# Loading the first layer's modulation weights by row blocks, four column groups at a time

## The chip, the cores and the metric

The kernel runs on one core of a Trainium2 chip. The metric is the time of one execution in microseconds of the device, median over runs. TensorE is called PE, VectorE DVE, ScalarE ACT, GpSimd POOL; SP (SyncE) computes nothing and issues most DMA transfers.

## The reference, cut to what matters

Two layers of a hybrid of attention, convolution and a linear recurrence over 1024 latent tokens, with a prefix of 256 context tokens, model width 1024. Only the entry of the first layer is touched:

```python
shift, scale, gate = split(silu(c) @ w_ada[0] + b_ada[0], 3)            # for the latent tokens
shift_c, scale_c, gate_c = split(silu(c_ctx) @ w_ada[0] + b_ada[0], 3)  # for the context
h  = layer_norm(x)   * (1 + scale)   + shift
hc = layer_norm(ctx) * (1 + scale_c) + shift_c
... = split_in_proj(h @ w_in[0])        # and the same of hc; gates: sigmoid(h @ w_gate + b_gate)
```

`w_ada[0]` is 1024 x 3072, all in 32-bit floats. The entry needs its first 2048 columns (shift and scale); the last 1024 are computed later, beside other work.

## The kernel before

Every product with `h` is done as three products of parts: `h` is cut into `hi` and `lo` (`hchi`, `hclo` for the context, `hlhi`, `hllo` for the latent tiles), each weight tile into `whi` (by ACT) and `wlo` (by DVE), and hi x hi, lo x hi, hi x lo are summed in PSUM. `h` is held transposed, model width on the partitions, in eight tiles of 128: `NT_C` (256 context tokens), `NT_0` and `NT_1` (512 latent tokens each).

`emit_h0` (L424) makes the first `h`. Its list `order` (L488) sets the sequence: `("a", g, q)` loads a block of `w_ada`, 256 rows by 512 columns (L437), and multiplies it with `cs`, the two vectors silu(c) and silu(c_ctx) as columns, into a PSUM tile `pa` of two rows (`ada_rows`, L442); after the fourth block of a column group `ada_fin` copies the two rows to SBUF (`arow`), turns them with 16 small matmuls in all against `sel`, and adds the bias into `ada[0]`. `("r",)` loads the eleven parameter rows (`load_rows`, L256) in SP's queue. `("x", i)` loads a tile of 128 tokens and normalizes it (`norm_x`: statistics on DVE, the power on POOL, `nb` on DVE, the scaling on ACT). `("m", nt, j)` modulates four of the eight tiles of `nt` (`modulate`, L459): transposes into `p0`, ACT writes `hf` with scale and shift, then `hi` by ACT or DVE, and `lo` by DVE.

`wcols` (L328) loads a weight of 1024 x 128 columns as 128 x 8 x 128, so in pieces of 512 B, and cuts it.

Behind `emit_h0` the streams of a layer (recurrence, attention, convolution, gates) are merged by a planner, `Driver`, which runs them by modelled costs and by the times at which it believes a thing ready. The tile framework then orders each engine's instructions, and the result is a fixed order on each engine. An engine takes its instructions in that order; a DMA queue too: an issue that waits holds up all that is behind it. DMA transfers share eight semaphores, taken in turn, so an issue also waits until an earlier transfer of the same semaphore has landed.

Of the kernel before, what the change touches and what calls it, by code (L numbers as in the profile page):

```python
# [17 lines left out]
D = 1024  # L18
# [21 lines left out]
LEAD = (2.0, 3.0, 1.5, 2.0)  # L40
SLACK = (1.0, 5.0, 2.0, 2.0)
MARGIN = (1.0, 3.0, 1.5, 0.0)
HOP = (0.2, 0.4, 0.1, 0.15)
PRIO = ((0, 1, 7, 3, 4, 5, 6, 8, 2), (1, 2, 8, 0, 4, 3, 6, 5, 7))
ROOM_SCORES = (3, 6)
# [144 lines left out]
def kernel(  # L190
# [23 lines left out]
    pad(H, 448, "padh1")  # L214
    pad(SM, 32, "pads")
    PR = ctx.enter_context(tc.tile_pool(name="padr", bufs=1, side="right"))
    pad(PR, 320, "padr")

    def f32(ap):
        return ap.bitcast(F32)  # L220
# [32 lines left out]
    P_ADA, P_GATE, P_CB, P_CG, P_CLB, P_LCW, P_LCB, P_BA, P_BX, P_LAM = 0, 24, 48, 52, 56, 60, 92, 100, 108, 116  # L253
    prm, cwt, drv = [], [], []

    def load_rows(l, get):  # L256
        ra, rb = get(), get()
        dve.memset(ra[96:128], 0.0)
        dve.memset(rb[96:128], 0.0)
        for off, n, src in (  # L260
            (P_ADA, 24, b_ada[l].rearrange("(r p) -> r p", p=128)),
            (P_GATE, 24, b_gate[l].rearrange("(r p) -> r p", p=128)),
            (P_CB, 4, conv_dw_b[l].rearrange("(r p) -> r p", p=128)),
            (P_CG, 4, conv_ln_g[l].rearrange("(r p) -> r p", p=128)),
            (P_CLB, 4, conv_ln_b[l].rearrange("(r p) -> r p", p=128)),
            (P_LCW, 32, lru_conv_w[l].rearrange("d k (r p) -> (d k r) p", p=128)),
            (P_LCB, 8, lru_conv_b[l].rearrange("d (r p) -> (d r) p", p=128)),
            (P_BA, 8, lru_b_a[l].rearrange("d (r p) -> (d r) p", p=128)),
            (P_BX, 8, lru_b_x[l].rearrange("d (r p) -> (d r) p", p=128)),
            (P_LAM, 8, lru_lambda[l].rearrange("d (r p) -> (d r) p", p=128)),  # L270
        ):
            sp.dma_start(out=ra[off:off + n], in_=src)
        sp.dma_start(out=rb[0:CK * 4], in_=conv_dw_w[l].rearrange("k (r p) -> (k r) p", p=128))
        return ra, rb

    def load_params(l, ra, rb):
# [65 lines left out]
    def wroom(n=1):  # L342
        return lambda: wlive[0] + n <= NW

    def wcols(src, o):
        return Wt(src[:, o:o + 128].rearrange("(k p) n -> p k n", p=128), KD, 128)
# [2 lines left out]
        act.activation(out=hi, in_=src, func=AF.Copy)  # L349
        dve.tensor_tensor(out=lo, in0=src, in1=f32(hi), op=ALU.subtract)  # L350

    cs = K.tile([128, KD, 2], F32, tag="cs", name="cs")
    csr = K.tile([128, KD, 4], F32R, tag="csr", name="csr")
    sel = K.tile([4, 2], F32, tag="sel", name="sel")
    dve.tensor_tensor(out=sel, in0=ident[0:4, 0:2], in1=ident[0:4, 2:4], op=ALU.add)

    def load_c():
        rows = SM.tile([128, 128], F32, tag="crow", name="crow")
        sp.dma_start(out=rows[0:8], in_=c[0].rearrange("(r p) -> r p", p=128))
        sp.dma_start(out=rows[8:16], in_=c_ctx.rearrange("(r p) -> r p", p=128))  # L360
# [58 lines left out]
    hT = {}  # L419

    def alloc_h(ti, n):
        tg, b = ("hc", 2) if n == 256 else ("hl", 4)
        return tuple(H.tile([128, KD, n], F32R, tag=tg, name=f"{tg}{v}", bufs=b) for v in ("hi", "lo"))

    def emit_h0(R, P):
        tiles = [(ctxt, 0), (ctxt, 128)] + [(x, 128 * i) for i in range(8)]
        raws, xt = {}, {}
        nts = (NT_C, NT_0, NT_1)

        def load_x(i):  # L430
            t = R.tile([128, 2, 512], F32, tag="raw0", name="x0", bufs=17).rearrange("p a b -> p (a b)")
            sp.dma_start(out=t, in_=tiles[i][0][0, tiles[i][1]:tiles[i][1] + 128, :])
            xt[i] = t

        def load_ada(g, q):
            raws[g, q] = R.tile([128, 2, 512], F32, tag="raw0", name="raw0", bufs=17)
            sp.dma_start(out=raws[g, q], in_=w_ada[0][q * 256:q * 256 + 256, g * 512:g * 512 + 512].rearrange(  # L437
                "(k p) n -> p k n", p=128))

        rows_ = {}  # L440

        def ada_rows(g, q):  # L442
            if q == 0:
                rows_[g] = P.tile([128, 512], F32, tag="p0", name="pa", bufs=4)
            for k in range(2):
                pe.matmul(out=rows_[g][0:2], lhsT=cs[:, q * 2 + k, :], rhs=raws[g, q][:, k, :],
                          start=(q == 0 and k == 0), stop=(q == 3 and k == 1))
            if q == 3:
                ada_fin(0, [g * 4 + i for i in range(4)], rows_[g], 2,
                        R.tile([128, 512], F32, tag="hf0", name="arow", bufs=5))  # L450
# [8 lines left out]
        def modulate(j, nt):  # L459
            ti, t0, n = nt  # L460
            s = 1 if ti == 0 else 0
            ps = P.tile([128, 512], F32, tag="p0", name="p0", bufs=4)
            for i in range(n // 128):
                pe.transpose(ps[:, i * 128:i * 128 + 128], xt[t0 // 128 + i][:, j * 128:j * 128 + 128], ident)
            hf = R.tile([128, 512], F32, tag="hf0", name="hf0", bufs=5)
            act.activation(out=hf[:, 0:n], in_=ps[:, 0:n], func=AF.Identity, scale=ada[0][:, 8 + j, s:s + 1],
                           bias=ada[0][:, j, s:s + 1])
            hi, lo = (v[:, j, :] for v in hT[0, ti])
            if j < (4, 4, 6)[ti]:
                act.activation(out=hi, in_=hf[:, 0:n], func=AF.Copy)  # L470
            else:
                dve.tensor_copy(hi, hf[:, 0:n])
            dve.tensor_tensor(out=lo, in0=hf[:, 0:n], in1=f32(hi), op=ALU.subtract)

        load_c()
        for nt in nts:
            hT[0, nt[0]] = alloc_h(nt[0], nt[2])
            if nt is NT_C:
                pad(H, 64, "padh2")

        def rows_tile():
            return R.tile([128, 128], F32, tag="rows", name="rows", bufs=2)

        order = [("a", 0, 0), ("a", 0, 1), ("a", 0, 2), ("r",), ("a", 2, 0), ("a", 0, 3), ("a", 2, 1), ("a", 2, 2),
                 ("a", 2, 3), ("x", 0), ("x", 1), ("a", 1, 0), ("a", 1, 1), ("a", 1, 2), ("a", 1, 3), ("a", 3, 0),
                 ("a", 3, 1), ("a", 3, 2), ("a", 3, 3), ("m", NT_C, 0), ("m", NT_C, 4), ("x", 2), ("x", 3),
                 ("x", 4), ("x", 5), ("x", 8), ("m", NT_0, 0), ("m", NT_0, 4), ("x", 6), ("x", 9), ("x", 7),
                 ("m", NT_1, 0), ("m", NT_1, 4)]  # L488
        for what, *v in order:
            if what == "m":  # L490
                for j in range(v[1], v[1] + 4):
                    modulate(j, v[0])
            elif what == "r":
                load_params(0, *load_rows(0, rows_tile))
            elif what == "a":
                load_ada(*v)
                ada_rows(*v)
            else:
                load_x(*v)
                norm_x(*v)  # L500

    class Pool_:

# [14 lines left out]
    def both(*conds):  # L518
        return lambda: all(c() for c in conds)

    def phase1(l, R, RH):
# [14 lines left out]
        def gemm_nt(w, nt, evac, wide=False):  # L536
            ti, t0, n = nt
            if wide and not state["lru"]:
                yield ("pe", w.ready)
                ps = psum2()  # L540
            else:
                yield ("pe", w.ready, lambda: pl_.used < (2 if state["lru"] else 3))
                pl_.take()
                wide = False
                ps = psum()
# [46 lines left out]

        def lru_in():
            for cc in range(4):
                yield ("pe", both(lambda: xgo[0] >= cc, wroom(), sl.room(), hl_.room(3)))
                w = wcols(w_in[l], O_XL + cc * 128)
                sl.take()
                hl_.take(3)
                lw_raw = half("lw_raw")
# [476 lines left out]

                yield from gating(0, j, get, 1.0)

        gorder = list(range(16, 24)) + list(range(8, 16)) + list(range(8))

        def gate_nt(w, j, nt):
            yield ("pe", w.ready, hl_.room())
# [8 lines left out]
            hl_.give()  # L1091

        def gates():
            ws = {}

            def fetch(i):
                if i < len(gorder) and i not in ws:
# [351 lines left out]
```

## Time and profile before

| | us |
|---|---|
| median of 3 runs | 2331.7 (2331.32 to 2335.34) |
| the profiled execution | 2330.59 |
| its span | 2328.8 |
| PE busy | 2268.0 (97%) |
| DVE busy | 1748.5 (75%) |
| ACT busy | 1067.1 (46%) |
| first product with `h` on PE begins at | 54.67 |

The granted clock is the share of TensorE's 2.4 GHz that it was given: 1.00, or 0.50 at the lower of its two levels; a mean between them is a stretch with both. Windows give the busy time of each engine in a stretch with its number of instructions. A 32-bit matmul stands as two records in the trace. The recorded duration of a matmul is longer than its step, as matmuls are pipelined: from start to start is what one costs in a row.

### The profile page before, as it was taken

The page shows a single profiled execution, that of the slowest core. Times are in us where ns is not written, and L with a number is a line of the kernel's source. Part 1 is how long each engine was busy: PE and PEld are TensorE (multiplying, and loading weights), DVE is VectorE, ACT ScalarE, POOL GpSimd, SP SyncE. Part 2 cuts the span into 40 slices and gives each one's busy share as a digit, 9 for nine tenths or more (in the row PEclk, how much of TensorE's full clock was granted, in tenths as well). Part 3 has the DMA queues.
Part 4 walks back from the last instruction along what each step waited for, and adds up shares of the span by engine and source line. Part 5 has one row for each costly group of instructions (what it writes and reads, how often), then busy time and mean ns, then how long its engine had stood idle before and what let it go on. Part 6 is the DMA issues. An engine that isn't in the chain of part 4 may idle for free.

```text
span 2328.8 us, 32221 instructions
## 1 busy us (share of the span) xinstructions
PE 2268.0 (97%) x12253; PEld 1921.6 (83%) x12253; DVE 1748.5 (75%) x2588; ACT 1067.1 (46%) x1702; POOL 91.4 (4%) x140
## 2 busy tenths in 40 slices
PE   7999999999999999999999999999999999999998
PEld 3888888888888887888988888888888878778988
DVE  5579967869859874448888839979778787657786
ACT  4555563244444575323444535665344456543231
POOL 1000000000000111000101000000000011000000
PEclk8999999999999999999999999999999999999999
DMA  7222323433334232567565522223433334348482
GB/s 279 70 75 98 118 75 121 138 116 109 100 120 132 84 102 88 189 214 226 169 223 176 187 70 66 75 90 128 140 93 96 91 118 136 109 135 279 136 280 73
DMA packets 305820, 309.91 MB, mean 133 GB/s; under 512 B 20609, under 2 KB 239617, under 8 KB 305665
## 3 DMA queue, kind: packets, MB, share of 16 engines
q1 hardware_dynamic: 277152, 255.94, 34.8%
q10 hardware_dynamic: 28512, 51.92, 6.3%
q8 instruction: 96, 1.57, 0.3%
q14 instruction: 60, 0.48, 0.1%
HBM read 232.92 MB, written 74.87 MB: 132 GB/s over the span
## 4 chain that ended last, share of the span: by engine, by line
PE 88%; DVE 6%; ACT 3%; DMA 2%; issue 2%; SPq 0%; POOLq 0%; POOL 0%; ACTq 0%; DVEq 0%
PE ps L73 81%; PE yp L73 3%; PE pt L73 2%; PE pa L73 1%; DVE wlo L73 1%; DVE acc L73 1%; DVE P L73 1%; ACT whi L73 1%; DVE pl L73 1%; DMA qd<-qd 0%; DVE xp L73 0%; PE p L73 0%; DMA raw<-in_w_out_dram 0%; ACT hf L73 0%; DVE st L73 0%
## 5 line engine op out<-in xcount | busy, mean ns | idle before, releaser
L73 PE MATMUL ps<-hlhi,whi 128*128 128x512 f32 x1728 | 681.4, 395 | 2.4 <-DVE gs L73 1.0
L73 PE MATMUL ps<-hlhi,wlo 128*128 128x512 f32 x1728 | 677.0, 392 | 2.0 <-DVE wlo L73 2.0
L73 PE MATMUL ps<-hllo,whi 128*128 128x512 f32 x1728 | 678.0, 392 | 0.1
L73 ACT ACTIVATE whi<-raw 128x1024 fp32r<-128x1024 f32 x240 | 253.9, 1058 | 433.6 <-PE ps L73 393.0
L73 DVE TENSOR_TENSOR wlo<-raw,whi 128x1024 fp32r<-128x1024 f32 x240 | 293.9, 1224 | 124.1 <-ACT whi L73 121.5
L73 PEld LDWEIGHTS ps<-hlhi,wlo 128*128 128x128 f32 x1728 | 325.5, 188 | 70.5 <-DVE wlo L73 2.9
L73 PEld LDWEIGHTS ps<-hlhi,whi 128*128 128x128 f32 x1728 | 326.1, 189 | 67.1 <-DVE pl L73 2.0
L73 PEld LDWEIGHTS ps<-hllo,whi 128*128 128x128 f32 x1728 | 325.8, 189 | 62.9 <-issue 0.7
L73 DVE SCALAR_TENSOR_TENSOR acc<-u,cwt,acc 128x1296 f32<-128x1296 f32 (+1 forms) x240 | 342.6, 1427 | 2.1
L73 PE MATMUL ps<-yh,whi 128*128 128x512 f32 (+1 forms) x480 | 175.6, 372 | 7.1 <-DVE thl L73 4.9
L73 PE MATMUL ps<-yl,whi 128*128 128x512 f32 (+1 forms) x480 | 176.3, 369 | 1.4 <-DVE yl L73 1.4
L73 PE MATMUL ps<-yh,wlo 128*128 128x512 f32 (+1 forms) x480 | 176.6, 369 | 0.0
L73 ACT ACTIVATE ph<-pt 128x512 fp32r<-128x512 f32 x160 | 93.9, 591 | 128.5 <-PE pt L73 126.7
L73 DVE TENSOR_TENSOR pl<-pt,ph 128x512 fp32r<-128x512 f32 x160 | 109.1, 686 | 50.9 <-ACT ph L73 49.4
L73 PE MATMUL ps<-whi,hlhi 128*128 128x256 f32 x512 | 144.3, 284 | 0.0
L73 PE MATMUL ps<-wlo,hlhi 128*128 128x256 f32 x512 | 144.0, 283 | 0.0
L73 PE MATMUL ps<-whi,hllo 128*128 128x256 f32 x512 | 142.6, 283 | 0.0
L73 ACT ACTIVATE P<-P,nm 128x640 f32<-128x640 f32 (+1 forms) x128 | 101.9, 797 | 81.3 <-DVE nm L73 81.2
L73 PE MATMUL ps<-hchi,whi 128*128 128x256 f32 x480 | 136.0, 283 | 2.0 <-ACT hchi L73 0.8
L73 PE MATMUL ps<-hchi,wlo 128*128 128x256 f32 x480 | 135.6, 282 | 1.0 <-DVE wlo L73 1.0
L73 PE MATMUL ps<-hclo,whi 128*128 128x256 f32 x480 | 134.8, 281 | 0.0
L73 DVE CUSTOM_DVE_ANT_0 P<-ps,m_mid,nsink 128x640 f32<-128x640 f32 (+1 forms) x112 | 93.2, 860 | 42.2 <-PE ps L73 40.7
(207 smaller groups left out, 3753.2 us busy)
## 6 DMA issues: line engine op xcount, KB each, us to landing
raw<-in_w_in_dram SPq DMA_DIRECT2D x60, 512.0 KB
raw<-in_w_branch_dram SPq DMA_DIRECT2D x60, 512.0 KB
raw<-in_w_ada_dram SPq DMA_DIRECT2D x48, 512.0 KB
raw<-in_w_gate_dram SPq DMA_DIRECT2D x48, 512.0 KB
th<-tg ACTq DMA_DIRECT2D x96, 256.0 KB
thl<-th SPq DMA_DIRECT2D x96, 256.0 KB
raw<-in_w_out_dram SPq DMA_DIRECT2D x40, 512.0 KB
yd<-gs ACTq DMA_DIRECT2D x48, 256.0 KB
```

The lines of the kernel that those rows point to most:

```text
L73: return f(*a, **k)
```

## The change

- The modulation weights of the first layer come in eight row blocks of 128 rows by 2048 columns (1 MiB, 8 KB in one piece a row) in place of sixteen blocks of 256 by 512. `cs` is padded to 32 columns, and each block is multiplied by four matmuls that write partitions 0, 32, 64 and 96 of one PSUM tile `pa` (`tile_position`). One copy (`arow`), four transposes and four additions make `ada[0]`.
- The parameter rows and c, c_ctx are loaded from ACT's queue.
- The context tiles are loaded first; once normalized they are transposed into PSUM and wait there, unmodulated.
- All x tiles have their own buffers; each group's loads and normalizings stand ahead of the modulation of the group before. The cut of `hi` moves from ACT to DVE in more tiles: (0, 2, 4) of eight by ACT in place of (4, 4, 6).
- The first gate weight and the first weight of the recurrence are loaded in `emit_h0`; the planner is told that the latent halves are ready at 12 and 24.

```diff
-    def load_rows(l, get):
+    def load_rows(l, get, queue=None):
+        queue = queue or sp
...
-            sp.dma_start(out=ra[off:off + n], in_=src)
+            queue.dma_start(out=ra[off:off + n], in_=src)
...
-    cs = K.tile([128, KD, 2], F32, tag="cs", name="cs")
+    csz = K.tile([128, KD, 32], F32, tag="cs", name="cs")
+    dve.memset(csz, 0.0)
+    cs = csz[:, :, 0:2]
...
-        sp.dma_start(out=rows[0:8], in_=c[0].rearrange("(r p) -> r p", p=128))
+        act.dma_start(out=rows[0:8], in_=c[0].rearrange("(r p) -> r p", p=128))
...
-            if j < (4, 4, 6)[ti]:
+            if j < (0, 2, 4)[ti]:
...
-        order = [("a", 0, 0), ("a", 0, 1), ("a", 0, 2), ("r",), ("a", 2, 0), ("a", 0, 3), ("a", 2, 1), ("a", 2, 2),
...
+        ra, rb = load_rows(0, lambda: R.tile([128, 128], F32, tag="rows", name="rows", bufs=2), act)
+        for i in range(2):
+            load_x(i)
+        pa = psum(name="pa")
+        raws = []
+        for q in range(KD):
+            raws.append(R.tile([128, 2048], F32, tag="raw0", name="raw0", bufs=5))
+            sp.dma_start(out=raws[q], in_=w_ada[0][q * 128:q * 128 + 128, 0:2048])
+            for g in range(4):
+                pe.matmul(out=pa[32 * g:32 * g + 32], lhsT=csz[:, q, :], rhs=raws[q][:, g * 512:g * 512 + 512],
+                          start=(q == 0), stop=(q == KD - 1), tile_position=(0, 32 * g))
+            if q == 0:
+                load_params(0, ra, rb)
+            elif q == 1:
+                for i in range(2):
+                    norm_x(i)
+                cps = [turn(NT_C, j) for j in range(KD)]
+        row = hf_tile("arow")
+        act.activation(out=row, in_=pa, func=AF.Copy)
+        pr = psum(name="pr")
+        for i in range(4):
+            pe.transpose(pr[:, i * 128:i * 128 + 128], row[:, i * 128:i * 128 + 128], ident)
+        for g in range(4):
+            bias = prm[0][:, P_ADA + 4 * g:P_ADA + 4 * g + 4].unsqueeze(2).to_broadcast([128, 4, 2])
+            dve.scalar_tensor_tensor(out=ada[0][:, 4 * g:4 * g + 4, :],
...
+        first_w["gate"] = wcols(w_gate[0], GATES[0] * 128)
+        first_w["lru"] = wcols(w_in[0], O_XL)
+        for i in range(2, 6):
+            load_x(i)
+        for j in range(KD):
+            modulate(NT_C, j, cps[j])
+        for i in range(2, 6):
+            norm_x(i)
...
+        hr[0, 1], hr[0, 2] = 12.0, 24.0
...
-                yield ("pe", w.ready)
+                yield ("pe", w.ready, hr.get((l, ti), 0.0))
```

What stands on three queues is set by the framework, and the diff does not show it. SP's queue at the start, before (`raw0` are blocks of `w_ada`, `rows` the parameter rows):

```order
L437 DMA raw0_188<-in_w_ada_dram 128x2x512
L437 DMA raw0_193<-in_w_ada_dram 128x2x512
L437 DMA raw0_197<-in_w_ada_dram 128x2x512
L272 DMA rows_201<-in_b_ada_dram 24x128
L272 DMA rows_201<-in_b_gate_dram 24x128
L272 DMA rows_201<-in_conv_dw_b_dram 4x128
L272 DMA rows_201<-in_conv_ln_g_dram 4x128
L272 DMA rows_201<-in_conv_ln_b_dram 4x128
```

SP's queue around the last blocks, now (`x0` are tiles of tokens, `raw` the gate and input weights):

```order
L488 DMA raw0_296<-in_w_ada_dram 128x2048
L444 DMA x0_173<-in_x_dram 128x1024
L444 DMA x0_174<-in_x_dram 128x1024
L444 DMA x0_175<-in_x_dram 128x1024
L488 DMA raw0_302<-in_w_ada_dram 128x2048
L444 DMA x0_176<-in_x_dram 128x1024
L444 DMA x0_177<-in_x_dram 128x1024
L444 DMA x0_178<-in_x_dram 128x1024
L488 DMA raw0_308<-in_w_ada_dram 128x2048
L331 DMA raw_654<-in_w_gate_dram 128x8x128
L331 DMA raw_674<-in_w_in_dram 128x8x128
```

The rows have left SP's queue, and the last three weight blocks stand behind all tiles of x; a second pair of weights stands behind the last block. ACT where the modulation begins, before:

```order
L73 ACTIVATE arow_325<-pa_310 2x512
L73 ACTIVATE hf0_335<-p0_332,ada0_160 128x256
L73 ACTIVATE hf0_342<-p0_339,ada0_160 128x256
L73 ACTIVATE x0_388<-x0_388,nb_398,rs_395 128x1024
L73 ACTIVATE hf0_349<-p0_346,ada0_160 128x256
L73 ACTIVATE hchi_180<-hf0_335 128x256
L73 ACTIVATE hchi_180<-hf0_342 128x256
L73 ACTIVATE x0_401<-x0_401,nb_411,rs_408 128x1024
```

and now:

```order
L74 ACTIVATE x0_176<-x0_176,nb_512,rs_509 128x1024
L74 ACTIVATE x0_177<-x0_177,nb_523,rs_520 128x1024
L74 ACTIVATE x0_178<-x0_178,nb_534,rs_531 128x1024
L74 ACTIVATE whi_656<-raw_654 128x1024
L74 ACTIVATE arow_314<-pa_216 128x512
L74 ACTIVATE whi_676<-raw_674 128x1024
L74 ACTIVATE hf0_341<-p0_258,ada0_161 128x256
L74 ACTIVATE hf0_345<-p0_258,ada0_161 128x256
```

All normalizing (`x0<-x0`) now stands ahead of the first `hf`, and two weight cuts have come between. DVE at the same place, before:

```order
L73 BN_STATS st_442<-x0_440 128x6 x2
L73 SCALAR_TENSOR_TENSOR ada0_160<-pa_310,prm0_219 128x8
L73 SCALAR_TENSOR_TENSOR nb_424<-mv_419,rs_421 128x1
L73 TENSOR_SCALAR rs_434<-mv_432 128x1
L73 BN_AGGR mv_445<-st_442 128x2
L73 TENSOR_TENSOR hclo_181<-hf0_335,hchi_180 128x256
```

and now:

```order
L74 TENSOR_TENSOR wlo_657<-raw_654,whi_656 128x1024
L74 TENSOR_TENSOR wlo_677<-raw_674,whi_676 128x1024
L74 SCALAR_TENSOR_TENSOR ada0_161<-pr_316,prm0_226 128x8 x4
L74 CAST hchi_191<-hf0_341 128x256
L74 TENSOR_TENSOR hclo_192<-hf0_341,hchi_191 128x256
```

The additions that make `ada` stood among the statistics of x; now they stand behind the low parts of the two weights.

## Rows read from the trace of the kernel before

**Rows 1.** PE's waits, 60 to 1100 us: total, times, longest; first and last of eleven.
```profile
PE yp L73 <- ACT ph L73: 6.3, 6, 2.2
...
PE ps L73 <- ACT arow L73: 0.2, 1, 0.2
```
**Rows 2.** Windows: length, busy PE, PEld, DVE, ACT, POOL, granted clock, DMA share, GB/s.
```profile
40.00:50.00 10.00, 5.60 (x28) 3.41 (x28) 7.89 (x25) 9.96 (x16) 1.80 (x4) 0.71 0.62 208
50.00:60.00 10.00, 8.28 (x47) 7.52 (x47) 7.98 (x23) 10.00 (x15) 2.29 (x3) 0.61 0.54 156
```
**Rows 3.** Timeline of PE: start, duration, operation, tiles, form, records [idle before].
```profile
13.63 7.03 PE L73 MATMUL pa<-raw,cs 128*2 128x512 f32 x16
...
53.05 1.97 PE L73 MATMUL p<-ident,x 128*128 128x128 f32 x8 [1.72 <-ACT hf L73]
54.67 0.57 PE L73 MATMUL ps<-hchi,whi 128*128 128x256 f32 x1
...
58.00 0.28 PE L73 MATMUL ps<-hchi,wlo 128*128 128x256 f32 x1
58.12 0.28 PE L73 MATMUL ps<-hchi,whi 128*128 128x256 f32 x1
...
59.54 1.03 PE L73 MATMUL p<-ident,x 128*128 128x128 f32 x8
60.33 0.36 PE L73 MATMUL ps<-hchi,whi 128*128 128x256 f32 x1
...
68.14 0.40 PE L73 MATMUL ps<-hlhi,wlo 128*128 128x512 f32 x1
68.37 0.39 PE L73 MATMUL ps<-hlhi,whi 128*128 128x512 f32 x1
```
**Rows 4.** PE's groups, 42 to 80 us; second and third stand for three each.
```profile
L73 PE MATMUL p<-ident,x 128*128 128x128 f32 x73 | 14.2, 332 | 5.8 <-ACT hf L73 3.9 <-ACT x L73 1.9
L73 PE MATMUL ps<-hchi,whi 128*128 128x256 f32 x24 | 7.4, 308 | 0.0
...
L73 PE MATMUL ps<-hlhi,whi 128*128 128x512 f32 x16 | 6.4, 403 | 0.0
```
**Rows 5.** Windows by what moved: weights, the hole, weights, tiles, gate weights.
```profile
3.70:7.80 4.10, 2.06 (x4) 0.52 (x5) 0.84 (x4) 1.27 (x3) 0.00 (x0) 1.00 1.00 374
7.80:11.20 3.40, 3.40 (x7) 0.51 (x5) 0.00 (x0) 0.00 (x0) 0.00 (x0) 1.00 0.16 34
20.00:30.00 10.00, 10.00 (x36) 3.35 (x35) 3.75 (x14) 2.96 (x3) 1.07 (x2) 1.00 1.04 388
32.00:38.00 6.00, 6.00 (x23) 2.06 (x22) 2.70 (x7) 0.01 (x1) 0.00 (x0) 1.00 1.03 406
38.50:41.50 3.00, 2.69 (x14) 1.19 (x12) 3.00 (x11) 1.46 (x4) 1.25 (x3) 1.00 1.21 303
```
**Rows 6.** Timeline of SP's queue: start, duration, what was issued.
```profile
1.18 0.37 SPq L359 DMA_DIRECT2D crow<-in_c_dram  x1
1.93 1.42 SPq L437 DMA_DIRECT2D raw<-in_w_ada_dram  x3
```
**Rows 7.** Timeline of DVE, columns as in Rows 3.
```profile
20.30 1.29 DVE L73 BATCH_NORM_STATS2 st<-x 128x6 f32<-128x512 f32 x2 [0.64 <-DMA x<-in_ctx_dram]
...
45.78 0.29 DVE L73 CAST hchi<-hf 128x256 fp32r<-128x256 f32 x1
...
47.51 1.22 DVE L73 TENSOR_TENSOR wlo<-raw,whi 128x1024 fp32r<-128x1024 f32 x1
```
**Rows 8.** Timeline of ACT, columns as in Rows 3.
```profile
40.04 0.59 ACT L73 ACTIVATE arow<-pa 2x512 f32<-2x512 f32 x1 [8.03 <-PE pa L73]
...
42.56 0.54 ACT L73 ACTIVATE hf<-p,ada 128x256 f32<-128x256 f32 x1
...
45.65 1.04 ACT L73 ACTIVATE whi<-raw 128x1024 fp32r<-128x1024 f32 x1
...
60.28 2.36 ACT L73 ACTIVATE x<-x,nb,rs 128x1024 f32<-128x1024 f32 x2
```

More of the change, by code (lines that the diff above doesn't have):

```diff
@@ L42 @@
 MARGIN = (1.0, 3.0, 1.5, 0.0)
+GATES = list(range(16, 24)) + list(range(8, 16)) + list(range(8))
 HOP = (0.2, 0.4, 0.1, 0.15)
@@ L216 @@
     PR = ctx.enter_context(tc.tile_pool(name="padr", bufs=1, side="right"))
-    pad(PR, 320, "padr")
+    pad(PR, 384, "padr")
     def f32(ap):
@@ L271, in load_rows @@
         ):
-            sp.dma_start(out=ra[off:off + n], in_=src)
-        sp.dma_start(out=rb[0:CK * 4], in_=conv_dw_w[l].rearrange("k (r p) -> (k r) p", p=128))
+            queue.dma_start(out=ra[off:off + n], in_=src)
+        queue.dma_start(out=rb[0:CK * 4], in_=conv_dw_w[l].rearrange("k (r p) -> (k r) p", p=128))
         return ra, rb
@@ L358, in load_c @@
         rows = SM.tile([128, 128], F32, tag="crow", name="crow")
-        sp.dma_start(out=rows[0:8], in_=c[0].rearrange("(r p) -> r p", p=128))
-        sp.dma_start(out=rows[8:16], in_=c_ctx.rearrange("(r p) -> r p", p=128))
+        act.dma_start(out=rows[0:8], in_=c[0].rearrange("(r p) -> r p", p=128))
+        act.dma_start(out=rows[8:16], in_=c_ctx.rearrange("(r p) -> r p", p=128))
         t = SM.tile([128, 128], F32, tag="crow2", name="crow2")
@@ L417, in ln_norm @@
         dve.tensor_scalar(out=dst, in0=src, scalar1=mv[:, 0:1], scalar2=rs[:, 0:1], op0=ALU.subtract, op1=ALU.mult)
-    hT = {}
+    hT, hr = {}, {}
     def alloc_h(ti, n):
@@ L423, in alloc_h, with hf_tile @@
         return tuple(H.tile([128, KD, n], F32R, tag=tg, name=f"{tg}{v}", bufs=b) for v in ("hi", "lo"))
+    first_w = {}
     def emit_h0(R, P):
         tiles = [(ctxt, 0), (ctxt, 128)] + [(x, 128 * i) for i in range(8)]
-        raws, xt = {}, {}
         nts = (NT_C, NT_0, NT_1)
-        def load_x(i):
[L431 to L450, printed above, removed]
+        xt, tp = {}, {}
+        for i in range(10):
+            xt[i] = R.tile([128, D], F32, tag="x", name="x0", bufs=10)
+        def hf_tile(name):
+            return R.tile([128, 512], F32, tag="hf0", name=name, bufs=4)
+        def load_x(i):
+            sp.dma_start(out=xt[i], in_=tiles[i][0][0, tiles[i][1]:tiles[i][1] + 128, :])
         def norm_x(i):
@@ L457, in norm_x, with turn, modulate @@
             act.activation(out=t, in_=t, func=AF.Identity, scale=rs, bias=nb)
-        def modulate(j, nt):
+        def turn(nt, j):
+            ti, t0, n = nt
+            per = 512 // n
+            if j % per == 0:
+                tp[ti, j // per] = P.tile([128, 512], F32, tag="p0", name="p0", bufs=4)
+            ps = tp[ti, j // per][:, j % per * n:j % per * n + n]
+            for i in range(n // 128):
+                pe.transpose(ps[:, i * 128:i * 128 + 128], xt[t0 // 128 + i][:, j * 128:j * 128 + 128], ident)
+            return ps
+        def modulate(nt, j, ps):
             ti, t0, n = nt
             s = 1 if ti == 0 else 0
[L462 to L466, printed above, removed]
+            hf = hf_tile("hf0")
+            act.activation(out=hf[:, 0:n], in_=ps, func=AF.Identity, scale=ada[0][:, 8 + j, s:s + 1],
                            bias=ada[0][:, j, s:s + 1])
             hi, lo = (v[:, j, :] for v in hT[0, ti])
-            if j < (4, 4, 6)[ti]:
+            if j < (0, 2, 4)[ti]:
                 act.activation(out=hi, in_=hf[:, 0:n], func=AF.Copy)
@@ L479, in emit_h0 @@
                 pad(H, 64, "padh2")
-        def rows_tile():
-            return R.tile([128, 128], F32, tag="rows", name="rows", bufs=2)
-        order = [("a", 0, 0), ("a", 0, 1), ("a", 0, 2), ("r",), ("a", 2, 0), ("a", 0, 3), ("a", 2, 1), ("a", 2, 2),
[L485 to L500, printed above, removed]
+        ra, rb = load_rows(0, lambda: R.tile([128, 128], F32, tag="rows", name="rows", bufs=2), act)
@@ new lines, in emit_h0 @@
+        row = hf_tile("arow")
[6 more added lines that the diff above has]
+            dve.scalar_tensor_tensor(out=ada[0][:, 4 * g:4 * g + 4, :],
+                                     in0=pr.rearrange("p (i g s) -> p i g s", g=4, s=32)[:, :, g, 0:2],
+                                     scalar=float(g // 2), in1=bias, op0=ALU.add, op1=ALU.add)
@@ new lines, in emit_h0 @@
+        first_w["gate"] = wcols(w_gate[0], GATES[0] * 128)
[6 more added lines that the diff above has]
+            norm_x(i)
+        for i in range(6, 10):
+            load_x(i)
+        for j in range(KD):
+            modulate(NT_0, j, turn(NT_0, j))
+        for i in range(6, 10):
+            norm_x(i)
+        for j in range(KD):
+            modulate(NT_1, j, turn(NT_1, j))
@@ L538, in gemm_nt @@
             if wide and not state["lru"]:
-                yield ("pe", w.ready)
+                yield ("pe", w.ready, hr.get((l, ti), 0.0))
                 ps = psum2()
             else:
-                yield ("pe", w.ready, lambda: pl_.used < (2 if state["lru"] else 3))
+                yield ("pe", w.ready, hr.get((l, ti), 0.0), lambda: pl_.used < (2 if state["lru"] else 3))
                 pl_.take()
@@ L594, in lru_in @@
             for cc in range(4):
-                yield ("pe", both(lambda: xgo[0] >= cc, wroom(), sl.room(), hl_.room(3)))
-                w = wcols(w_in[l], O_XL + cc * 128)
+                yield ("pe", both(lambda: xgo[0] >= cc, lambda: "lru" in first_w or wroom()(), sl.room(), hl_.room(3)))
+                w = first_w.pop("lru", None) or wcols(w_in[l], O_XL + cc * 128)
                 sl.take()
@@ L1077, in att_out @@
                 yield from gating(0, j, get, 1.0)
-        gorder = list(range(16, 24)) + list(range(8, 16)) + list(range(8))
+        gorder = GATES
         def gate_nt(w, j, nt):
@@ L1093, in gates @@
         def gates():
-            ws = {}
+            ws = {0: first_w.pop("gate")} if l == 0 else {}
             def fetch(i):
```

## The prediction

> **What bounds the kernel now.** I read PE's waits first, then the windows of the first 60 us, then the timelines of the queues and engines there. From 60 to 1100 us PE waits in all 15.7 of 1040 us, eleven rows of which the largest is 6.3 [rows 1]: nearly all of the program is a row of matmuls that waits for nothing, so the change can pay by letting that row begin earlier, or by the gaps in it. The beginning is where PE lacks work: from 40 to 50 us it is busy 5.60 of 10 us at a mean granted clock of 0.71, from 50 to 60 us 8.28 at 0.61, while ACT is full [rows 2]. The reader is to see there that PE waits for ACT, which normalizes and modulates h, that the clock has fallen to its lower level for most of that time, and that the first product with h starts at 54.67 us [rows 3].
>
> What the old start is worth is one number, and I work it out backwards. From 42 to 80 us PE does 72 matmuls of 256 columns (three groups of 24), 46 of 512 (16, 15, 15) and 73 transposes, of which 64 belong to the latent tiles [rows 4]. At the full clock these step at 0.12, 0.23 and 0.10 us from start to start (58.00 to 58.12, 68.14 to 68.37, 59.54 to 60.33 for eight) [rows 3]: 72 x 0.12 + 46 x 0.23 + 64 x 0.10 = 25.6 us. PE is never idle after 60 us, so the old program stands as if a full-speed run had begun at 80 - 25.6 = **54.4 us**. The same number for the new program, taken from 54.4, is the gain.
>
> **The change part by part.**
>
> *The loads.* Before, SP issues three blocks of weights and then the eleven parameter rows, each of which waits until an earlier transfer has landed; from 7.8 to 11.2 us only 34 GB/s move, against 374 ahead of it [rows 5]. The rows now stand in ACT's queue, and that hole of 3.4 us closes, unless they hold the stream up from there (a rival). The Trainium skill speaks against a gain (DMA: Bandwidth & Descriptors, Rules for kernel authors): spreading transfers over SP and ACT brings no bandwidth, since the same 16 engines serve both, and only saves issue time. The row shows a queue that waits, not engines that are full, and I go by the row.
>
> What has to land up to the last weight block is 28 pieces of 0.524 MB: 2 context tiles, 8 latent tiles, 8 blocks of two pieces, one gate weight and one weight of the recurrence. The rates are 406 GB/s for the tiles' 4 KB rows, 388 for the old 2 KB weight pieces, 303 where the 512 B pieces of gate weights run [rows 5]. 5.24 MB / 406 = 12.9; 8.39 / 388 = 21.6; 1.05 / 303 = 3.5; together 38.0 us. The new 8 KB pieces have no row; priced as 4 KB they give 37.1, the other end; I keep 388. Bulk data flowed at 3.7 [rows 5], some 1.8 us after its first issue at 1.93; the first context tile now takes the place that `crow` had, 1.18 [rows 6], so 3.0. A waiter sees a landing about 0.7 us later: the first statistics waited until 20.30 for a context tile [rows 7] whose bytes, by the rates, were there at 19.6. So the last weight block is seen at 3.0 + 38.0 + 0.7 = **41.7** (40.8 at the other end), the last latent tile, one block ahead of it, at 39.0, and the second pair of weights, behind it in the queue, at 43.4 and 45.1.
>
> *The modulation matmuls.* Eight took 7.0 us [rows 3], 0.87 each, 32 in all. The same 32 remain, four to a block, and no row shows four column groups side by side. For the last block the bounds are 0.9 us (all four at once, full clock) and 7.0 (one by one at half the clock); one by one at the full clock is 3.5. I take the range from 0.9 to 3.5, which the next step makes one case. The Trainium skill (TensorEngine Tiling (Array Packing), Key Properties) lets tiles work in parallel; by that alone the case of 7.0 would fall away, and no run here shows it yet.
>
> *What is late next.* The order shows it. On ACT there stand behind the loads, in this order, the three last normalizings of x, `whi_656`, `arow`, `whi_676`, and only then the first `hf`; on DVE `wlo_657` and `wlo_677` stand ahead of the four `ada` additions. So the modulation is queued behind two weights that land after the last block. The sum: statistics of the last tile 39.4 to 40.6 (0.4 for small operations ahead, 1.2 for the pair [rows 7]); `nb` of the third last tile is behind them, 40.9; three normalizings at 1.13 (two take 2.36 with their overlap [rows 8]), 44.3; `whi` 1.04, 45.3; `arow` 0.59, 45.9, if the last block's matmuls end by 45.3, that is within 3.6 us; `whi_676` to 46.9 [rows 8]; `wlo_677` 1.22, 48.1; four additions of 8 columns, 0.5 together (each is less than the cast's 0.29), 48.6; `hf` 0.54 [rows 8]; the cast of `hchi` 0.29 [rows 7]: the first product at **49.5 us** in place of 54.67. The four transposes of `arow`, in place of 16 small matmuls, lie beside `whi_676`.
>
> *The clock.* PE has little to do from 42 us on, so the products start at the lower level, as before. There PE ran without a gap from 53.05, its first product stood at 54.67, and the step was the full one by 58.0 [rows 3]: 3.3 to 4.9 us at half speed, 1.7 to 2.5 of them lost. I take 2.0. The new run is worth a start at 51.5.
>
> *Behind it.* ACT has eight `hf` of 0.54 at most and then the latent halves; DVE, which now casts all eight context tiles, needs 0.29 for each and about as much for `hclo`; PE needs 0.7 us (1.4 at half the clock) for the six products of one tile and has the transposes of the latent tiles between, so PE ends last there and no gap is added. Eight normalizings at 1.2, which stood among the `hf` before, made the room.
>
> Sum: 54.4 - 51.5 = **2.9 us** earlier; ends 3.8 (8 KB pieces at the tiles' rate) and -0.5 (matmuls one by one at half clock, 3.4 later).
>
> *The rest of layer 0.* The planner now holds two loaded weights and due times of 12 and 24 for the latent halves, and so the order of layer 0's first phase changes throughout; from the last products of that phase to the end of the program it is the old one. The work is the same, the gaps need not be. In the new order the attention's first scores stand behind 1,991 matmuls instead of 2,189; fewer of its second products `yp` stand directly behind the transposes whose copies `ph` they need, and more have only 0.5 to 1.2 us of matmuls between. No row prices that: the bounds are the 15.7 us [rows 1] all gone, or doubled. I take 0, since neither sign has the better reason.
>
> So 2330.6 (the profiled execution, span 2328.8) - 2.9 = 2327.7; the median of the runs lies 1.1 above the profiled one: **2328.8 us**.
>
> **The rivals.**
>
> *The new order closes gaps.* With half of the 15.7 us gone the time is 2328.8 - 7.9 = 2320.9. For it: the attention starts sooner, so more other products can stand between its steps. It is faster by 0.2% (4.7 us, about what a measurement of this kernel can tell from no change) from 1.8 us of closed gaps on. 0.30.
>
> *The new order opens them* (the other side): `yp` waits for `ph`, up to 2.2 us a time, 6.3 in all [rows 1]; with the attention's waits growing until the 15.7 are doubled the time is 2344.5. It is slower than 2336.4 from 7.6 us of added waits on. For it: more places with little work between. Against it: the planner works by the same costs as before. 0.18.
>
> *The start gains nothing*: the four groups run one by one at half clock (first product at 52.9), or the rows in ACT's queue hold up the stream by the old 3.4 us, as SP's transfers of x and of the last three blocks each wait for one of them (the same time). Either makes it 0.5 us later than before, 2332.2. The skill's rule on queues would be this case too. Against the second: SP comes to those transfers some 20 us in, long after the rows can be there. 0.12.
>
> **How the numbers follow.** The forecast has 0.40, with a range of its own from 2327 to 2331; with the third rival, no change within 0.2% has 0.52, faster 0.30, slower 0.18. The range takes in the gap-closing case to its price and the gap-opening one to 10 us of added waits: 2320 to 2339.
>
> **What would show it.** In the new profile: no stretch under 100 GB/s between 4 and 40 us; the last block's matmuls near 42 us, and whether four take 0.9, 1.8, 3.5 or 7 us; `arow` behind a `whi` near 45; the first product with h near 49.5, the full clock some 3 to 5 us later; by the work done at 80 us a start worth 51.5. I am wrong if the first product stands after 53 us, if `arow` waits for PE, or if PE's waits from 60 to 1100 us differ by more than 5 us from 15.7.

## The result, and the profile after

The changed kernel takes 2352.2 us (median of 4 runs, 2345.3 to 2353.7) against 2332.2 us for the kernel before: a ratio of 1.0082, interval 1.0066 to 1.0097. It is slower by 20 us, outside the predicted range of 2320 to 2339 us. The profiled execution has a span of 2351.4 us, 22.6 more than before.

The start came nearly as forecast. Timelines of three engines, of the kernel after (start, duration, engine, operation, tiles, form, records, idle time before; they answer [rows 3, 7, 8]):

```profile
21.07 1.92 PE L74 MATMUL pa<-raw,cs 128*32 128x512 f32 x16
...
42.64 1.93 PE L74 MATMUL pa<-raw,cs 128*32 128x512 f32 x8 [5.46 <-DMA raw<-in_w_ada_dram]
46.54 1.12 PE L74 MATMUL pr<-ident,arow 128*128 128x128 f32 x4 [1.96 <-ACT arow L74]
49.98 0.77 PE L74 MATMUL ps<-hchi,whi 128*128 128x256 f32 x2 [2.33 <-DVE hchi L74]
...
55.23 0.28 PE L74 MATMUL ps<-hclo,whi 128*128 128x256 f32 x1
```
```profile
44.96 1.04 ACT L74 ACTIVATE whi<-raw 128x1024 fp32r<-128x1024 f32 x1
45.91 0.57 ACT L74 ACTIVATE arow<-pa 128x512 f32<-128x512 f32 x1
46.38 1.04 ACT L74 ACTIVATE whi<-raw 128x1024 fp32r<-128x1024 f32 x1
```
```profile
48.61 0.38 DVE L74 SCALAR_TENSOR_TENSOR ada<-pr,prm 128x8 f32<-128x8 f32 x4
```

The first product with h stands at 49.98 us instead of 54.67, and PE steps at full speed from 55.2. The work done by 80 us, counted as for [rows 4], is 72 matmuls of 256 columns, 53 of 512 and 64 transposes (groups of PE from 42 to 80 us; name, form, records, busy time, mean ns, idle time):

```profile
L74 PE MATMUL p<-ident,x 128*128 128x128 f32 x64 | 10.3, 290 | 0.0
L74 PE MATMUL ps<-hclo,whi 128*128 128x256 f32 x24 | 8.0, 331 | 0.0
...
L74 PE MATMUL ps<-hlhi,whi 128*128 128x512 f32 x18 | 7.3, 406 | 0.0
L74 PE MATMUL ps<-hllo,whi 128*128 128x512 f32 x18 | 7.2, 399 | 0.0
L74 PE MATMUL ps<-hlhi,wlo 128*128 128x512 f32 x17 | 6.7, 396 | 0.0
```

72 x 0.12 + 53 x 0.23 + 64 x 0.10 = 27.2 us, a start worth 52.8 against 54.4 before: 1.6 us gained.

The loss comes behind it. The first product of phase 2 of layer 0 (`ps<-yh`; from there on the two programs have the same order, but for a few matmuls some 2,000 us in) stands in the timeline of PE 20.1 us later, first before, then after:

```profile
1021.45 0.39 PE L73 MATMUL ps<-yh,whi 128*128 128x512 f32 x1
```
```profile
1041.58 0.39 PE L74 MATMUL ps<-yh,whi 128*128 128x512 f32 x1
```

PE's waits from 60 to 1100 us, after (total, times, longest), which answer [rows 1]:

```profile
PE ps L74 <- ACT tg L74: 5.4, 4, 2.7
PE pt L74 <- ACT P L74: 3.9, 1, 3.9
PE ps L74 <- ACT arow L74: 3.4, 4, 1.3
PE yp L74 <- ACT ph L74: 2.1, 2, 1.3
...
PE ps L74 <- DVE xl L74: 0.2, 1, 0.2
```

The sixteen rows sum to 26.3 us, 10.6 more than before. That is half of the loss. The other half is in the granted clock. PE's windows around some of these waits, after (length, busy time, granted clock, DMA share, GB/s):

```profile
150.00:160.00 10.00, 10.00 (x51) 1.00 0.23 65
160.00:170.00 10.00, 8.72 (x48) 0.83 0.42 117
250.00:260.00 10.00, 7.37 (x26) 0.83 0.43 144
440.00:450.00 10.00, 5.11 (x23) 0.72 0.40 132
```

From 160 to 170 us PE waits once, 1.28 us, and the window's clock is 0.83, so 3.4 of its 10 us stood at the half level (1.2 GHz), which costs another 1.7 us of work. From 80 us to the first product of phase 2 the trace's clock records hold 13.7 us at the half level before and 34.1 us after: 20.5 us more, worth 10.2. So the first phase lost 10.6 (waits) + 10.2 (clock) - 0.7 = 20.1 us. The 0.7 is what is left over: by the work already done at 80 us it should be 1.6, so 0.9 us stays unexplained. Phase 2 of layer 0 is longer by 1.3 and layer 1 by 1.1.

Why PE waits: ACT takes its work in order, and in the new order some copies that PE needs stand behind weight cuts that are themselves waiting. ACT's timeline, after, ahead of the waits at 163.7 (for `arow`) and 252.6 (for `tg`):

```profile
160.42 1.06 ACT L74 ACTIVATE whi<-raw 128x1024 fp32r<-128x1024 f32 x1 [4.21 <-DMA raw<-in_w_in_dram]
162.31 1.06 ACT L74 ACTIVATE whi<-raw 128x1024 fp32r<-128x1024 f32 x1 [0.82 <-DMA raw<-in_w_in_dram]
163.27 0.36 ACT L74 ACTIVATE arow<-ps 4x256 f32<-4x256 f32 x1
...
248.35 1.06 ACT L74 ACTIVATE whi<-raw 128x1024 fp32r<-128x1024 f32 x1 [7.11 <-PE ps L74]
249.32 1.26 ACT L74 ACTIVATE kh<-pj 64x512 fp32r<-64x512 f32 x2
250.60 1.28 ACT L74 ACT_TABLE_LOAD   x1
251.89 0.69 ACT L74 ACTIVATE tg<-ps,drv 128x512 f32<-128x512 f32 x1
```
```profile
163.68 0.60 PE L74 MATMUL ps<-sel,arow 4*128 4x2 f32 x4 [1.28 <-ACT arow L74]
...
252.63 0.50 PE L74 MATMUL ps<-hlhi,whi 128*128 128x512 f32 x1 [2.67 <-ACT tg L74]
```

At 248.35 a weight cut had waited 7.1 us for products of PE; two copies and a table load of 1.28 us follow, and only then the `tg` that PE waits for.

This accounts for the four waits for `arow`, all behind a weight cut, and for the longest for `tg`, but not for all. The longest wait of all, 3.85 us at 443.83 for `P`, has its cause on DVE, whose order is fixed too. ACT, then DVE, ahead of it:

```profile
443.27 0.51 ACT L74 ACTIVATE P<-P,es 128x256 f32<-128x256 f32 x1 [2.89 <-DVE es L74]
```
```profile
440.45 1.22 DVE L74 TENSOR_TENSOR wlo<-raw,whi 128x1024 fp32r<-128x1024 f32 x1
441.59 1.56 DVE L74 SCALAR_TENSOR_TENSOR acc<-u,cwt,acc 128x1296 f32<-128x1296 f32 x1
443.07 0.17 DVE L74 RECIPROCAL es<-es 128x4 f32<-128x4 f32 x1
```

The small reciprocal that `P` needs stands behind a weight's low part and a step of the convolution, which take 2.6 us; nothing there waits.

### The profile page after: what moved, and what is told of

Same layout as the page of the kernel before. It is cut to its first block, busy times and chain, and to the rows that moved or that the text cites. A ratio compares the mean times of both kernels' runs of the same rounds, so it can differ in the third digit from the quotient of the medians.

```text
span 2351.4 us, 32147 instructions
## 1 busy us (share of the span) xinstructions
PE 2258.2 (96%) x12225; PEld 1923.7 (82%) x12225; DVE 1749.8 (74%) x2597; ACT 1066.4 (45%) x1691; POOL 89.0 (4%) x140
## 4 chain that ended last, share of the span: by engine, by line
PE 86%; DVE 6%; DMA 3%; ACT 2%; issue 2%; SPq 0%; POOLq 0%; POOL 0%; ACTq 0%; DVEq 0%
PE ps L74 81%; PE yp L74 3%; PE pt L74 2%; DVE wlo L74 1%; DVE acc L74 1%; DMA raw<-in_w_in_dram 1%; DMA thl<-th 1%; DVE st L74 1%; DMA qd<-qd 1%; DVE P L74 1%; DVE pl L74 0%; ACT whi L74 0%; DVE xp L74 0%; DMA raw<-in_w_ada_dram 0%; PE p L74 0%
```

## The experiments

All kernels but 8 and 12 are in one table; each ratio goes by runs of before beside it (medians 2332.2 to 2334.8). "First phase" is the first product of phase 2 of layer 0; waits and time at half clock are PE's from 80 us to there, of one profiled execution; "like before" counts the places, of 5,130 in that phase, at which the same kind of product stands as in the kernel before.

| kernel | like before | median us | ratio to before (interval) | first phase | waits | half clock |
|---|---|---|---|---|---|---|
| before | 5,130 | 2332.2 | | 1021.5 | 16.0 | 13.7 |
| after | 983 | 2352.2 | 1.0082 (1.0066 to 1.0097) | 1041.6 | 26.6 | 34.1 |
| 1 new start, old order | 4,934 | 2333.5 | 1.0000 (0.9991 to 1.0009) | 1020.0 | 15.1 | 10.2 |
| 2 old start, new order | 1,029 | 2351.7 | 1.0078 (1.0064 to 1.0092) | 1040.1 | 27.6 | 27.3 |
| 3 no due times | 1,103 | 2338.3 | 1.0017 (1.0007 to 1.0026) | 1024.0 | 20.1 | 10.2 |
| 4 no early weights | 1,023 | 2352.0 | 1.0079 (1.0062 to 1.0096) | 1036.8 | 28.6 | 20.5 |
| 5 moved buffers | 5,130 | 2333.2 | 0.9999 (0.9990 to 1.0008) | 1022.1 | 15.6 | 13.7 |
| 6 as 1, old places | 4,934 | 2333.0 | 0.9996 (0.9987 to 1.0005) | 1022.8 | 17.1 | 13.7 |
| 7 due at 12 and 12 | 3,979 | 2334.3 | 1.0005 (0.9995 to 1.0014) | 1020.0 | 16.3 | 13.7 |
| 9 due at 12 and 23 | 3,974 | 2332.6 | 0.9990 (0.9981 to 1.0000) | 1020.7 | 15.5 | 17.1 |
| 10 due at 10 and 22 | 4,246 | 2331.4 | 0.9989 (0.9980 to 0.9997) | 1020.8 | 16.7 | 13.7 |
| 11 due at 18 and 36 | 2,521 | 2342.9 | 1.0042 (1.0029 to 1.0055) | 1029.2 | 20.3 | 20.5 |

In every row the length from 80 us less the waits less half of the time at half clock is nearly the same, 916.6 to 919.7 us: the work does not change, and what an order costs is its waits and the clock behind them. With the traces of 8 and 12 taken in, this remainder is 918.1 us on average with the new start (nine traces) and 919.5 with the old (five). So about 1.4 of the 1.6 us gained at the start are still there, but single traces scatter by more than that.

The change holds three things: the new start (loads, column groups, turns), the two weights loaded ahead (`first_w`), and the planner's due times (`hr`). The first four runs take them apart.

**1. New start, old order.** `first_w` out and the due times 0:

```diff
-        first_w["gate"] = wcols(w_gate[0], GATES[0] * 128)
-        first_w["lru"] = wcols(w_in[0], O_XL)
-        hr[0, 1], hr[0, 2] = 12.0, 24.0
+        hr[0, 1], hr[0, 2] = 0.0, 0.0
-            ws = {0: first_w.pop("gate")} if l == 0 else {}
+            ws = {}
```

> The changed kernel, but the two first weights are loaded by their own streams again and the planner is told no due times for the latent halves: the new start stays, and the products of layer 0's first phase stand again in the order of before at 4,934 of 5,130 places. If the order made the loss: 2330.6 us, that is before's 2332.2 less the 1.6 us that the new start is worth by the work done at 80 us, within 2 us; PE's waits from 80 us to the first product of phase 2 near 16 us, and half clock there near 13.7 us. If the new start or the moved buffers made it: near 2350 us, with PE waits there near 26 us.

Measured 2333.5 against 2333.1 for before beside it. The loss is gone, and so are its waits. But the gain of 1.6 us isn't there at the end either: the time is 0.9 us over the upper end that was expected, which went by an earlier median of before, 2332.2. The first phase ended 1.5 us earlier, with 0.9 us less of waits and 3.4 less at half clock, and phase 2 of layer 0 took 2.9 longer; experiments 5 and 6 ask why.

**2. Old start, new order.** The kernel before; the only edit is the due times in `gemm_nt`:

```diff
-    hT = {}
+    hT, hr = {}, {(0, 1): 12.0, (0, 2): 24.0}
-                yield ("pe", w.ready)
+                yield ("pe", w.ready, hr.get((l, ti), 0.0))
-                yield ("pe", w.ready, lambda: pl_.used < (2 if state["lru"] else 3))
+                yield ("pe", w.ready, hr.get((l, ti), 0.0), lambda: pl_.used < (2 if state["lru"] else 3))
```

> The kernel before, with its own start; only the planner is told the due times of 12 and 24 for the latent halves. Its products of layer 0's first phase then stand as in the changed kernel at 4,335 of 5,130 places. If the order made the loss: 2353 us (2348 to 2358), PE's waits from 80 us to the first product of phase 2 near 26 us, half clock there near 34 us. If the new start or the moved buffers made it: 2332 us, since neither is here.

2351.7 us: two numbers told to the planner cost the kernel before the whole loss, with nothing of the new start in it. The waits are for the same tiles as in the changed kernel. Half clock came to 27.3 us where 34 was expected. PE's largest rows here, 60 to 1100 us:

```profile
PE pt L73 <- ACT P L73: 6.7, 2, 3.9
PE ps L73 <- ACT tg L73: 5.4, 4, 2.7
...
PE ps L73 <- ACT arow L73: 2.2, 4, 0.9
```

The row of `tg` is that of the changed kernel to the tenth.

**3. No due times**, early weights kept: `hr` is 0 and 0 in the changed kernel.

> The changed kernel without the due times of 12 and 24; the two first weights stay loaded ahead. The products stand in a third order, like neither (1,103 places of 5,130 in common with before, 1,119 with the changed kernel). If the order's waits and the clock they cost are the whole loss, whatever this order brings: time = 2330.6 + (waits - 16.0) + (half clock - 13.7) / 2, with both counted from 80 us to the first product of phase 2, to within 2 us. If the due times alone are the cause: 2331 us. If the early weights are: 2350 us.

2338.3 us, between the two: a third order with waits of its own. The sum expected gives 2330.6 + 4.1 - 1.7 = 2333.0; the profiled execution took 2335.0, at the edge of the 2 us. The median lies 3 us above that: six of the ten runs took 2337.2 to 2341.5, and there is no trace of those. So the due times carry most of the loss, and loading the weights early also picks an order.

**4. No early weights**, due times kept: the `first_w` lines of experiment 1 alone.

> The changed kernel without the two early weights; the due times of 12 and 24 stay. The products stand as in the changed kernel at 4,847 of 5,130 places. If the due times made the bad order: 2352 us (2346 to 2357). If the early weights did: 2331 us.

2352.0 us: without the early weights the loss is whole.

**5. Moved buffers.** The kernel before with 960 B of pad behind `cs` and 384 B on the right:

```diff
-    pad(PR, 320, "padr")
+    pad(PR, 384, "padr")
+    pad(K, 960, "padk")
```

> The kernel before, start and order unchanged, with every buffer behind the constants 960 B higher, and the pad on the right 384 B, as in the changed kernel. If the moved buffers cost what experiment 1 lost again behind layer 0's first phase: 2336 us (before's 2333.1 and the 2.9 that phase 2 of layer 0 was longer there), with PE's waits for thl in that phase near 8 us. If addresses do nothing: 2333.1 within 1.5 us, waits for thl near 5.

2333.2 us, and PE waits 4.1 us for `thl` in phase 2: the moved buffers cost nothing that these runs can tell (ratio 0.9990 to 1.0008).

**6. New start, old places.** Experiment 1 with the padded columns in the start's own pool:

```diff
-    pad(PR, 384, "padr")
+    pad(PR, 320, "padr")
...
-    csz = K.tile([128, KD, 32], F32, tag="cs", name="cs")
-    dve.memset(csz, 0.0)
-    cs = csz[:, :, 0:2]
+    cs = K.tile([128, KD, 2], F32, tag="cs", name="cs")
...
+        csz = R.tile([128, KD, 32], F32, tag="csz", name="csz")
+        dve.memset(csz, 0.0)
+        dve.tensor_copy(csz[:, :, 0:2], cs)
```

> Experiment 1 with the padded silu columns in the start's own pool, so that all later buffers lie where they lay before. If the moved buffers cost 3 us: 2330.5 us, faster than before by the 1.5 us that the first phase ended earlier in experiment 1 and more. If the start's gain is given back to a stretch that waits for transfers whatever the addresses are: 2333 us, with phase 2 of layer 0 longer by what the first phase ended earlier.

2333.0 us against 2333.2, and here the first phase ended 1.3 us later than in before, so the second half of that expectation isn't met as it stands: executions of one order differ by more in this phase (1020.0 and 1022.8 in experiments 1 and 6) than the start is worth. What repeats is the wait for `thl` in phase 2 of layer 0: 7.0 to 8.9 us in each of the nine kernels with the new start, 2.7, 3.5, 4.1, 5.2 and 7.1 in the five with the old one, though the order of that phase is nearly the same. From its first to its last product with `yh`, phase 2 of layer 0 takes 279.3 us on average with the new start and 277.9 with the old: it gives back about what the first phase has gained. Why is open.

**7. Due at 12 and 12**, the rest as in experiment 1.

> Experiment 1 with due times of 12 for both latent halves in place of none. The products stand as in before at 3,979 of 5,130 places. If it is the due time of 24 for the second half that makes the order with the many waits: 2333 us (2329 to 2338), waits from 80 us to the first product of phase 2 under 20 us. If any due time that binds makes it: 2343 us or more, waits over 23 us.

2334.3 us with waits of 16.3. A due time that changes the order is harmless as such.

**8. Six waits, first try.** In the kernel before PE turns a tile, ACT copies it eight times, and PE turns the copy, at six places of phase 2 of layer 1:

```diff
+                            if last and dch == 4:
+                                q = psum(name="q")
+                                nc.tensor.transpose(q[:, 0:128], ident, ident)
+                                t = SM.tile([128, 128], F32, tag="crow", name="hold")
+                                for _ in range(8):
+                                    nc.scalar.activation(out=t, in_=q[:, 0:128], func=AF.Copy)
+                                nc.tensor.transpose(q[:, 0:128], t, ident)
```

> The kernel before with six added waits in phase 2 of layer 1, where PE waits for nothing in before (978 matmuls from the first to the last product with y): PE turns a tile, ACT copies it eight times, PE turns the copy. Each should keep PE idle some 2 us. If a wait costs its clock as well, each is followed by a stretch at half clock of 3.4 us, in which 1.7 us are lost, and the phase grows by the six waits and 10 us: about 23 us in all. If a wait costs only itself: by 13 us, with the clock at 1.00.

It tested nothing: 2335.0 us, and PE waited for nothing there, since the framework put other products between the two turns (timeline of PE):

```profile
2109.15 0.27 PE L1240 MATMUL q<-ident 128*128 128x128 f32 x1
...
2117.00 0.27 PE L1244 MATMUL q<-ident,hold 128*128 128x128 f32 x1
```

**9. Due at 23.** The changed kernel with one number changed:

```diff
-        hr[0, 1], hr[0, 2] = 12.0, 24.0
+        hr[0, 1], hr[0, 2] = 12.0, 23.0
```

> The changed kernel with everything in it, early weights and due times too, and one number changed: the second latent half is due at 23 instead of 24. From 23 on down to 12 the planner makes one and the same order, with 3,974 places of 5,130 as in before, and 1,270 as in the changed kernel. If the loss is the order that the planner happens to make at 24: 2333.5 us (2330 to 2337), 18 us less than the changed kernel, PE's waits from 80 us to the first product of phase 2 under 20 us. If early weights and due times together are the cause, whatever the order: 2345 us or more.

2332.6 us, 19.6 less than the changed kernel for one step of one due time. PE's waits, 60 to 1100 us, are again those of [rows 1] in kind, `yp` for `ph` ahead, and that for `tg` is back at 0.6:

```profile
PE yp L74 <- ACT ph L74: 3.9, 6, 1.1
...
PE ps L74 <- ACT tg L74: 0.6, 2, 0.3
```

The windows that stood at 0.83, 0.83 and 0.72 are whole:

```profile
160.00:170.00 10.00, 10.00 (x60) 1.00 0.47 136
250.00:260.00 10.00, 10.00 (x56) 1.00 0.30 92
440.00:450.00 10.00, 10.00 (x66) 1.00 0.60 186
```

**10. Due at 10 and 22**, the rest of the change kept.

> The same with 10 and 22, which gives a further order (4,246 places as in before). If an order near that of before is a good one: 2333 us (2329 to 2338). If each order has its own waits and likeness to before says nothing: anywhere from 2330 to 2352, and the time is 2333.5 + (waits - 16.0) + (half clock - 13.7) / 2 within 2 us, both counted from 80 us to the first product of phase 2.

2331.4 us, ratio 0.9989 (0.9980 to 0.9997): the best of the study, though by less than 0.2%. The sum gives 2334.2, 1.7 above the profiled execution, so within the 2 us, and 2.8 above the median, so outside them.

**11. Due at 18 and 36**, the rest as in experiment 1.

> Experiment 1 (no early weights) with due times of 18 and 36, later than the changed kernel's. The order has 2,521 places as in before, 1,061 as in the changed kernel. If late due times starve the planner: more than the changed kernel's 2352 us. If the due time only picks an order, and orders differ by luck: 2333 to 2345 us, by its own waits and half clock as in experiment 10.

2342.9 us, by its waits and clock 2341.2. A later due time costs less than 24: there is no trend, only one order or another.

**12. Forced waits.** The kernel before; ACT copies the first rows of the merged y onto themselves, which every column block behind needs first:

```diff
                         yield ("pe", wa[1].ready)
+                        if last and t == 0 and qd == qds[0] and qd:
+                            for _ in range(9):
+                                nc.scalar.activation(out=mg[0][:, 0, 0:n], in_=f32(mg[0][:, 0, 0:n]), func=AF.Copy)
```

> The kernel before; in phase 2 of layer 1, where PE waits for nothing in before, ACT copies the first 128 rows of the merged y onto themselves nine times at five places between the column blocks of w_out, so that every product behind must wait. 45 copies of about 0.5 us; at each place the copies begin some 2.8 us ahead of the end of PE's work and keep it idle 2 us. If a wait costs its clock as well: five stretches at half clock of 3.4 us, and a phase longer by 10 us of waits and 8.5 us of clock, 18.5 in all. If it costs only itself: 10 us and a clock of 1.00.

2369.7 us. The waits came out at 5.0 us each, not 2: a copy took 0.65 us, and weight cuts stood between the copies. Timeline of PE at the first place, then windows (length, busy time of the five engines, granted clock, DMA share, GB/s):

```profile
2181.89 0.58 PE L73 MATMUL ps<-whi,hlhi 128*128 128x256 f32 x1 [5.00 <-ACT hlhi L1286]
...
2182.49 0.41 PE L73 MATMUL ps<-whi,hllo 128*128 128x256 f32 x1
2182.70 0.41 PE L73 MATMUL ps<-whi,hlhi 128*128 128x256 f32 x1
...
2188.11 0.28 PE L73 MATMUL ps<-whi,hllo 128*128 128x256 f32 x1
2188.23 0.28 PE L73 MATMUL ps<-whi,hlhi 128*128 128x256 f32 x1
```
```profile
2172.00:2177.00 5.00, 4.89 (x41) 4.68 (x40) 2.60 (x7) 2.68 (x5) 0.00 (x0) 1.00 0.08 30
2177.00:2182.00 5.00, 0.11 (x1) 0.11 (x1) 2.61 (x4) 4.68 (x8) 0.00 (x0) 0.75 0.53 162
2182.00:2187.00 5.00, 5.00 (x26) 5.00 (x27) 0.01 (x1) 0.00 (x0) 0.00 (x0) 0.57 0.15 51
```

Behind the wait the same matmuls step at 0.21 us, and from 2186.3 on at 0.12 again. From its first product with y to its end the stretch takes 270.4 us instead of 233.4, 37.0 more, of which 25.2 are the five waits: the clock took 11.8 us, 2.4 a wait. In the clock records each of the five stretches at the half level is 6.8 us long, not 3.4, and begins while PE still waits. A wait of this length that nothing covers costs itself and then the clock.

## Why the prediction was wrong, step by step

**The start: right in its chain, 1.3 us short in its worth.** The chain on ACT and DVE ran in the order of the sum and 0.4 to 0.7 us later: `whi` ended at 46.0, `arow` at 46.5, the second `whi` at 47.4, the additions at 49.0, where 45.3, 45.9, 46.9 and 48.6 were put; the first product stood at 49.98 instead of 49.5. The last block was seen at 42.64 (41.7 forecast) and its four matmuls took 1.93 us at the half clock, inside the one case from 0.9 to 3.5. No stretch under 100 GB/s is left while the blocks and tiles load: the hole of [rows 5] has 430 GB/s in its place (window of the kernel after):

```profile
8.00:12.00 4.00, 2.23 (x13) 0.45 (x15) 1.09 (x8) 0.22 (x1) 1.07 (x2) 1.00 1.03 430
```

The rates up to 42 us, 379 to 430 GB/s, are near those of [rows 5]; the second queue carried only the small rows. As far as such small loads can show it, the trace agrees with the Trainium skill (DMA: Bandwidth & Descriptors, Rules for kernel authors) that a second issuing queue brings no bandwidth and saves only issue time. But "each of which waits" was a misreading of the hole: of the eleven rows before, three waited for a landing, 2.6 us in all (waits of SP's queue in the kernel before, 0 to 12 us), and issuing the eleven took 3.4 us (0.25 to 0.44 each), so the larger part was issue time:

```profile
SPq L272 <- DMA raw<-in_w_ada_dram: 2.6, 3, 1.3
```

The term of the clock was mis-sized: half speed lasted from 49.98 to 55.2, 5.2 us where 3.3 to 4.9 were taken, with 2.6 lost instead of 2.0. Together 1.6 us were gained instead of 2.9 (0.5 less by the later product, 0.6 by the clock, 0.2 not accounted for). Whether any of it reaches the end of the program is not settled: the new start with nearly the old order measures as before (experiments 1 and 6), while the whole change with other due times comes out 0.1% ahead (experiments 9 and 10, 2.3 and 3.4 us, intervals up to 1.0000 and 0.9997). So the third rival, a start that gains nothing, is about right for experiments 1 and 6, but by neither of its two mechanisms.

**The rest of layer 0: the step that failed.** It was set to 0, "since neither sign has the better reason", with the 15.7 us of [rows 1] gone or doubled as its bounds. The order was seen to change throughout, and that was right; the term was +20.8 us, 10.6 of waits and 10.2 of clock, and experiments 2 and 9 show that the order alone makes it. Two things were missing. First, the price: an uncovered us of waiting was taken to cost 1 us. The waits grew by 10.6, within the doubling, but brought 20.5 us at half clock, another 10.2. Before's own trace had it: the longest of the six waits of `yp` for `ph`, 2.2 us up to 593.9, has a stretch of 3.4 us at the half level behind it, and from 80 us to phase 2 there were 13.7 us at half clock beside 16.0 of waits. A window behind that wait, before (length, busy time of the five engines, granted clock, DMA share, GB/s):

```profile
594.00:597.00 3.00, 3.00 (x7) 2.38 (x8) 3.00 (x5) 0.83 (x3) 0.00 (x0) 0.50 0.57 168
```

With the clock costing as much again, the doubling would have ended at 2328.8 + 31.4 = 2360 us. Second, nothing bounds the waits of a new order by those of the old one; the doubling was a choice, and that the waits stayed within it was luck.

**The rival on the other side: right in sign, wrong in place.** It named `yp` waiting for `ph`; that row fell from 6.3 to 2.1. The growth is in `tg` (0.6 to 5.4), `arow` (0.2 to 3.4) and the turns of `P` (none to 3.9): PE waiting for copies on ACT that stand late in ACT's or DVE's order, behind weight cuts above all. That "the planner works by the same costs as before" was offered against it and was no reason: its costs were the same in experiment 9 and in the changed kernel, 20 us apart.

**The rival with closed gaps** did not come in any order here by more than 0.9 us of waits (15.1 against 16.0). Before's order is a good one among those seen: those of the other inputs have 15.5 to 28.6.

**That neighbouring orders could be compared beforehand** was missed. The planner's result for 12 and 23 is 3,974 places like before, for 12 and 24 it is 983; one step in an input, and the phase is another program. Such a step says that the term is a draw, and the range has to be as wide as the draws are: 2331 to 2352 in this study.

## What to carry to other kernels

Where a planner makes the order, a changed due time or an early load is a new draw of the whole order: compare the order for neighbouring inputs, and time several, before crediting or blaming the edit itself. Price a wait of an otherwise full TensorE with the stretch at half clock behind it; here that about doubled the cost of waits of 0.2 to 3.9 us, and added half to those of 5 us. When PE waits for a copy that should have been ready, read the other engine's queue ahead of the copy: here something stood there that waited itself, or that took long.

## What the runs showed of the hardware

Four column groups run side by side: two blocks of four matmuls took 1.92 us at 21.07, 0.96 a block, where one such matmul took 0.87 in [rows 3]; at the half clock a block took 1.93 (42.64). (The trace's clock records begin at 21.07 us, so the 1.00 that a window ahead of it shows, as that of 8 to 12 us above, is no measurement; the blocks there took 1.94 each.) The time of four side by side agrees with the Trainium skill (TensorEngine Tiling (Array Packing), Key Properties), and the case of 7.0 us falls away. The stretches at half clock at or behind PE's waits, from 60 us until the last few us of the program, are 3.4 or 6.8 us long in the clock records of every trace here. A single wait of 1.28 us (163.7, after) has one behind it, and not every wait does: 1.07 us at 798.5, after, has none, and neither has the one of 1.77 us at 570.0 in the kernel before.
